# Gated merge of the two mixers with the activations stationary and tokens on partitions

## The chip, the core and the metric

The kernel runs on one core of a Trainium2 chip. The metric is the device time of one execution in microseconds (us); runs of one kernel are given by their median. TensorE is called PE, its weight load PEld, VectorE DVE, ScalarE ACT; SP is the queue that issues the transfers.

## The reference

One transformer block on x of 256 tokens by 2048 features, in f32. What matters here:

```python
z = h @ w_in                                  # h: normed and modulated x
q, kc, vc, ks, vs, kw, vw, g_nsa, lx, ly, ga, gb = jnp.split(z, ...)
o_a = nsa_attention(...)                      # 256 x 2048
o_b = jax.nn.gelu(ly) * rg_lru(u, ...)        # 256 x 2048
merged = jax.nn.sigmoid(ga) * (o_a @ proj_a) + jax.nn.sigmoid(gb) * (o_b @ proj_b)
return merged @ w_out
```

The merge is four products of 256 x 2048 by 2048 x 2048 (ga, gb, and the two projections), two sigmoids, two multiplications and a sum. The modulation vector behind h comes from `ada_w`, 96 pieces of 1 MB.

## The kernel before, in words

Every f32 product is made of three products of a faster format: both operands are split into a rounded part (hi) and the rest (lo), and hi hi, hi lo and lo hi are added in PSUM. An activation tile holds both parts side by side, 256 tokens of hi and 256 of lo, features on partitions. Weights come in 1 MB pieces through a ring of four `raw` tiles (`stage`, L97); ACT rounds each half piece (1024 columns) into `hi` (L107) and DVE writes the rest into `lo` (L108). There are three buffers of `hi` and three of `lo`, so a half piece is split while PE works three halves earlier. A half piece is 12 or 16 matmuls on PE.

Three forms of product matter. `dense_pair` (L114) holds 128 x 128 blocks of weights in the array and streams activations: the hi block sees 512 columns (256 tokens' hi and lo, L130), the lo block 256 (L131); the two 256-wide halves of the PSUM bank are added by DVE in `reduce` (L226). Its result has features on partitions. `dense_tok` (L191) holds 128 tokens of the activations and streams 512 columns of weights: three matmuls of 512 (L202 to L204). Its result has tokens on partitions and needs no `reduce`; `w_out` and `w_down` use it. `dense_pair1` (L171) is a form of three matmuls of 256 (L184 to L187), used by the recurrent mixer (LRU) ahead of the merge.

The first third of the program is made of passes over contraction blocks (`SPANS`, four of them): in each pass `tiles_of` (L408) adds a few blocks of the contraction to twelve output tiles, because h itself is still being made. Blocks 8 and 9 (`VB`) are products with tokens on partitions (L419 to L421); all others, the two gate blocks `mq` (10 and 11) among them, are three matmuls of 256 columns (L426 to L428). `out_of` (L430) adds each pass to the SBUF tile. The `mq` blocks are the first 512 columns of ga and gb.

The merge (L735 to L758) runs over eight groups of 256 columns. For each mixer s it makes the gate (`dense_pair` of `w_gates`, or `mq` for the first two groups), its sigmoid, the projection (`dense_pair` of `w_proj`), and the product of both; the sum is split into `mg` (features on partitions), which `dense_tok` of `w_out` (L789) reads as the stationary side. Behind each mixer come one or two `filler` pieces: a 1 MB piece of `ada_w` is loaded into the same ring and DVE multiplies and sums it (L233, then a short L234). `to_row` (L264) is a small transpose.

The order on each engine is set when the program is built, by a scheduler with a model of time; the transfers on SP stay in the order of the code. At run time an engine takes its instructions strictly in that order, each waiting for its semaphores.

Of the kernel before, what the change touches and what calls it, by code (L numbers as in the profile page):

```python
# [5 lines left out]
F32 = mybir.dt.float32  # L6
F32R = mybir.dt.float32r
BF16 = mybir.dt.bfloat16
AF = mybir.ActivationFunctionType
ALU = mybir.AluOpType  # L10
# [3 lines left out]
T = 256  # L14
# [24 lines left out]
def block_kernel(tc, x_t, x_n, gf_row, cols_d, consts_d, ada_w, w_kv0, w_kv, w_v, w_gate, w_q, cmp_w, cmp_w2,  # L39
# [16 lines left out]
    with ExitStack() as es:  # L56
# [167 lines left out]
        def reduce(out_ap, p):  # L224
            with tc.high_priority(200):
                V.tensor_reduce(out_ap, p.rearrange("p (a b) -> p b a", a=2), axis=AX, op=ALU.add)  # L226
# [23 lines left out]
        for c in range(4):  # L250
            p = bank()
# [137 lines left out]

        held = {}  # L390

        mq = [big.tile([128, 4, T], F32, tag="M%d" % n, name="mq") for n in range(2)]

        blocks = [(w_kv[i], kvc[i] if i < 2 else kT[:, i - 2]) for i in range(4)]
        blocks += [(w_q[i], qT[i]) for i in range(4)]
        blocks += [(w_v[b], vN[:, b]) for b in range(2)]
        blocks += [(w_mq[i], mq[i]) for i in range(2)]
        KV, Q, VB, MQ = range(4), range(4, 8), range(8, 10), range(10, 12)

        def banks_of(i, q):  # L400
            if i > 1:
# [6 lines left out]
        def tiles_of(i, ps, hi, lo, c0, kt, q):  # L408

            k0, k1 = SPANS[q] if i > 1 else (0, KT)  # L410
            first, last = kt == k0, kt == k1 - 1
            if q == 2 and i > 3 and i % 2:
                first, last = kt == k1 - 2, kt == k1 - 3
            if i in VB:
                wh, wl = hi[:, c0:c0 + 512], lo[:, c0:c0 + 512]
                for j in range(2):
                    xh = h1[:, kt, j * 128:j * 128 + 128]
                    xl = h1[:, kt, 256 + j * 128:256 + j * 128 + 128]
                    PE.matmul(ps[j], xh, wh, start=first, stop=False, skip_group_check=True)  # L419
                    PE.matmul(ps[j], xh, wl, start=False, stop=False, skip_group_check=True)  # L420
                    PE.matmul(ps[j], xl, wh, start=False, stop=last, skip_group_check=True)  # L421
                return
            for f in range(4):
                o = ps[f // 2][:, (f % 2) * 256:(f % 2) * 256 + 256]
                sl = slice(c0 + f * 128, c0 + f * 128 + 128)
                PE.matmul(o, hi[:, sl], h1[:, kt, 0:256], start=first and f % 2 == 0, stop=False, skip_group_check=True)  # L426
                PE.matmul(o, hi[:, sl], h1[:, kt, 256:512], start=False, stop=False, skip_group_check=True)  # L427
                PE.matmul(o, lo[:, sl], h1[:, kt, 0:256], start=False, stop=last, skip_group_check=True)  # L428

        def out_of(i, ps, q):  # L430
            if i < 2 and q < 3:
                return
            for j in range(2):
                dst = blocks[i][1]
                if i in VB:
                    v, d = ps[j], dst[:, j]
                else:
                    v, d = ps[j].rearrange("p (f t) -> p f t", f=2), dst[:, 2 * j:2 * j + 2]
                if q == 0 or i < 2:
                    A.activation(d, v, AF.Copy)  # L440
                else:
                    V.tensor_tensor(d, v, d, op=ALU.add)
# [34 lines left out]
        def filler(n=1):  # L477
            for _ in range(n):
                if fill:
                    m, kt = fill.pop(0)  # L480
                    ada_piece(crow, ada_w[m, kt], m * 16 + kt)
# [250 lines left out]
        for n in (4, 5):  # L732
            m2 = big.tile([128, 2, 2, 512], F32R, tag="D%d" % n, name="mg2")
            mg += [m2[:, 0], m2[:, 1]]
        for gr in range(8):  # L735
            m = []
            for s, rhs in ((0, lambda kt: oA[:, kt]), (1, lambda kt: oB[kt // 2][:, kt % 2])):
                if gr < 2:
                    sg = mq[s][:, 2 * gr:2 * gr + 2]
                else:  # L740
                    ps = dense_pair([w_gates[gr - 2, s, k] for k in range(2)], h1r)
                    sg = tmp.tile([128, 2, 256], F32, tag=("r", "iu")[s], bufs=1, name="sg")
                    for f in range(2):
                        reduce(sg[:, f], ps[f])
                A.activation(sg, sg, AF.Sigmoid)
                ps = dense_pair([w_proj[gr, s, k] for k in range(2)], rhs)
                pv = tmp.tile([128, 2, 256], F32, tag="tt", bufs=1, name="pv")
                for f in range(2):
                    reduce(pv[:, f], ps[f])
                V.tensor_tensor(sg, sg, pv, op=ALU.mult)  # L750
                m.append(sg)
                filler(1 if gr < 2 else 2)
            if gr == 5:
                row1 = to_row(32)
            V.tensor_tensor(m[0], m[0], m[1], op=ALU.add)
            oh = mg[gr][:, :, 0:256]
            A.activation(oh, m[0], AF.Copy)
            V.tensor_tensor(mg[gr][:, :, 256:512], m[0], oh.bitcast(F32), op=ALU.subtract)  # L758
        filler(max(0, len(fill) - 16))


# [120 lines left out]
def _pack(w, c=256, k=8):  # L882
    K, N = w.shape
    return np.ascontiguousarray(w.reshape(K // (128 * k), k, 128, N // c, c).transpose(3, 0, 2, 1, 4)).reshape(
        N // c, K // (128 * k), 128, k * c)
# [19 lines left out]
def _layout(i):  # L905
    f = {k: np.asarray(v) for k, v in i.items()}
    a = {}
    a["x_t"] = np.ascontiguousarray(f["x"][0].T.reshape(KT, 128, T).transpose(1, 0, 2))
    a["x_n"] = np.ascontiguousarray(f["x"][0].reshape(2, 128, D).transpose(1, 0, 2))
    a["gf_row"] = f["final_g"]  # L910
    parts = [_colv(f["c"]), _colv(f["ada_b"]), _colv(f["norm1_g"]), _colv(f["norm2_g"]),
             _colv(f["lru_conv_b"]), _colv(f["lru_conv_w"]), _colv(f["lru_ba"]), _colv(f["lru_bi"]),
             _colv(f["lru_lambda"]), _colv(f["ffn_conv_b"]), _colv(f["ffn_conv_w"]), 
             np.full((128, 1), EPS, np.float32), np.eye(128, dtype=np.float32)]
    cols = np.zeros((128, NCOLS), np.float32)
    cols[:, :_off] = np.concatenate(parts, axis=1)
    a["cols"] = cols
    qp = np.arange(128)
    causal = np.where(qp[None, :] <= qp[:, None], 0.0, NEG)
    vis = (np.arange(NCMP) * 16 + 31)[None, :] <= np.arange(T)[:, None]  # L920
    vis4 = np.repeat(vis.reshape(2, 128, 1, NCMP), 4, axis=2).transpose(1, 0, 2, 3).reshape(128, 120)
    a["consts"] = np.concatenate([causal, np.where(vis4, 0.0, NEG), vis4.astype(np.float64)],
                                 axis=1).astype(np.float32)
    a["consts"] = np.concatenate([a["consts"], f["cmp_pos_k"][0].T, f["cmp_pos_v"][0].T], axis=1)
    ada = f["ada_w"][0]
    a["ada_w"] = np.ascontiguousarray(ada.T).reshape(6, KT, 128, D)
    a["ada_w"][1, 0] = ada[:, D:D + 128].reshape(KT, 128, 128).transpose(1, 0, 2).reshape(128, D)
    w = f["w_in"][0]
    kv = np.concatenate([w[:, 2048:3072], w[:, 3072:3584], w[:, 4096:4608]], axis=1)
    a["w_kv0"] = kv[:256].reshape(2, 128, 2048)  # L930
    a["w_kv"] = _blocks(kv)
    a["w_v"] = _blocks(np.concatenate([w[:, 3584:4096], w[:, 4608:5120]], axis=1))
    a["w_gate"] = np.ascontiguousarray(w[:, 5120:5168].reshape(KT, 128, 48).transpose(1, 0, 2)).reshape(128, 768)
    a["w_q"] = _blocks(w[:, 0:2048])
    a["cmp_w"] = np.stack([np.ascontiguousarray(f[n][0].transpose(1, 0, 2)).reshape(128, 4096)
                           for n in ("cmp_w1_k", "cmp_w1_v")])
    a["cmp_w2"] = np.stack([f["cmp_w2_k"][0], f["cmp_w2_v"][0]], axis=1)
    a["w_lru"] = np.concatenate([_pack(w[:, 5168:7216]), _pack(w[:, 7216:9264])])
    lw = np.stack([f["lru_wa"][0], f["lru_wi"][0]], axis=1).reshape(4, 4, 2, 128, 128)
    a["lru_w"] = np.ascontiguousarray(lw.transpose(0, 3, 1, 2, 4)).reshape(4, 128, 1024)  # L940
    ga, gb = w[:, 9264:11312], w[:, 11312:13360]
    a["w_mq"] = np.concatenate([_blocks(ga[:, :512]), _blocks(gb[:, :512])])
    a["w_gates"] = np.stack([_pack(ga[:, 512:]), _pack(gb[:, 512:])], axis=1)
    a["w_proj"] = np.stack([_pack(f["proj_a"][0]), _pack(f["proj_b"][0])], axis=1)
    a["w_out"] = _tok(f["w_out"][0])
    up = f["ffn_up"][0]
    a["w_up"] = np.stack([_pack(up[:, :DFF]).reshape(2, 12, 2, 128, 2048),
                          _pack(up[:, DFF:]).reshape(2, 12, 2, 128, 2048)], axis=2)
    dn = f["ffn_down"][0]
    a["w_down"] = np.stack([_tok(dn[:DFF // 2]), _tok(dn[DFF // 2:])])  # L950
    return {k: np.ascontiguousarray(v) for k, v in a.items()}
# [17 lines left out]
```

## Time and profile before

| | us |
|---|---|
| median of 3 runs (1819.79 to 1822.76) | 1820.9 |
| the profiled execution, its own time | 1822.74 |
| its span, from the first to the last instruction | 1820.9 |
| PE busy | 1799.7 (99%) |
| DVE busy | 1372.0 (75%) |
| ACT busy | 868.2 (48%) |

The profiled execution lies 1.8 us above the median. PE counts as busy from the start of a matmul to its modelled end, so matmuls that overlap count once, and the rate of the work is read from the starts of matmuls, not from busy time. The merge stands from about 600 to 922 us of the span, `w_out` from 919 to 1009, the passes from about 30 to 340.

### The profile page before, as it was taken

The page shows a single profiled execution, that of the slowest core. Times are in us where ns is not written, and L with a number is a line of the kernel's source. Part 1 is how long each engine was busy: PE and PEld are TensorE (multiplying, and loading weights), DVE is VectorE, ACT ScalarE, POOL GpSimd, SP SyncE. Part 2 cuts the span into 40 slices and gives each one's busy share as a digit, 9 for nine tenths or more (in the row PEclk, how much of TensorE's full clock was granted, in tenths as well). Part 3 has the DMA queues.
Part 4 walks back from the last instruction along what each step waited for, and adds up shares of the span by engine and source line. Part 5 has one row for each costly group of instructions (what it writes and reads, how often), then busy time and mean ns, then how long its engine had stood idle before and what let it go on. Part 6 is the DMA issues. An engine that isn't in the chain of part 4 may idle for free.

```text
span 1820.9 us, 27160 instructions
## 1 busy us (share of the span) xinstructions
PE 1799.7 (99%) x10952; PEld 1586.8 (87%) x10952; DVE 1372.0 (75%) x1990; ACT 868.2 (48%) x1168; POOL 0.2 (0%) x4
## 2 busy tenths in 40 slices
PE   8999999999999999999999999999999999999998
PEld 7999998788999888888888998888888888888886
DVE  7998866888788877777766898888654677777555
ACT  5644534655578444444445554444433444444443
POOL 0000000000000000000000000000000000000000
PEclk9999999999999999999999999999999999999999
DMA  9999862555756677777776566777655555555553
GB/s 350 371 332 349 316 237 103 193 201 185 253 204 229 248 262 281 284 279 283 283 263 208 172 225 244 259 280 277 254 193 200 185 185 187 187 191 190 194 186 114
DMA packets 64206, 429.60 MB, mean 236 GB/s; under 512 B 7088, under 2 KB 7376, under 8 KB 15568
## 3 DMA queue, kind: packets, MB, share of 16 engines
q1 hardware_dynamic: 63792, 427.08, 66.3%
q8 instruction: 86, 1.41, 0.3%
q10 hardware_dynamic: 288, 0.79, 0.1%
q14 instruction: 40, 0.33, 0.1%
HBM read 425.72 MB, written 2.11 MB: 235 GB/s over the span
## 4 chain that ended last, share of the span: by engine, by line
PE 96%; DVE 1%; ACT 1%; issue 1%; DMA 1%; DVEq 0%; ACTq 0%
PE P L130 29%; PE P L131 15%; PE P L204 6%; PE P L202 6%; PE P L203 6%; PE P L426 3%; PE P L428 3%; PE P L427 3%; PE P L184 3%; PE P L187 3%; PE P L186 3%; PE P L148 1%; PE P L147 1%; PE P L149 1%; PE s L621 1%; PE oT L651 1%
## 5 line engine op out<-in xcount | busy, mean ns | idle before, releaser
L107 ACT ACTIVATE hi<-raw 128x1024 fp32r<-128x1024 f32 x589 | 623.4, 1060 | 812.1 <-PE P L130 401.3
L108 DVE TENSOR_TENSOR lo<-raw,hi 128x1024 fp32r<-128x1024 f32 x589 | 717.3, 1221 | 368.5 <-ACT hi L107 367.2
L130 PE MATMUL P<-h,hi 128*128 128x512 f32 x1728 | 599.9, 396 | 0.0
L131 PE MATMUL P<-h,lo 128*128 128x256 f32 x1728 | 468.2, 280 | 0.0
L130 PEld LDWEIGHTS P<-h,hi 128*128 128x128 f32 x1728 | 318.0, 188 | 69.2
L131 PEld LDWEIGHTS P<-h,lo 128*128 128x128 f32 x1728 | 326.0, 189 | 8.8
L233 DVE SCALAR_TENSOR_TENSOR raw<-raw,crow 128x2048 f32<-128x2048 f32 x64 | 146.2, 2284 | 1.8 <-DMA raw<-ada_w 1.7
L184 PE MATMUL P<-h,hi 128*128 128x256 f32 x512 | 146.8, 287 | 0.7 <-ACT hi L107 0.7
L187 PE MATMUL P<-h,lo 128*128 128x256 f32 x512 | 147.3, 288 | 0.1
L186 PE MATMUL P<-h,hi 128*128 128x256 f32 x512 | 146.9, 287 | 0.0
L426 PE MATMUL P<-h,hi 128*128 128x256 f32 x512 | 144.0, 285 | 0.0
L427 PE MATMUL P<-h,hi 128*128 128x256 f32 x512 | 143.4, 284 | 0.0
L428 PE MATMUL P<-h,lo 128*128 128x256 f32 x512 | 137.3, 284 | 0.0
L187 PEld LDWEIGHTS P<-h,lo 128*128 128x128 f32 x512 | 97.9, 191 | 3.3 <-issue 2.5
L184 PEld LDWEIGHTS P<-h,hi 128*128 128x128 f32 x512 | 97.9, 191 | 2.3 <-ACT hi L107 1.3
L426 PEld LDWEIGHTS P<-h,hi 128*128 128x128 f32 x512 | 98.5, 192 | 0.4
L186 PEld LDWEIGHTS P<-h,hi 128*128 128x128 f32 x512 | 97.9, 191 | 1.1 <-issue 1.0
L427 PEld LDWEIGHTS P<-h,hi 128*128 128x128 f32 x512 | 98.5, 192 | 0.1
L428 PEld LDWEIGHTS P<-h,lo 128*128 128x128 f32 x512 | 94.5, 192 | 1.6 <-issue 1.5
L203 PE MATMUL P<-lo,ua 128*128 128x512 f32 x240 | 93.4, 389 | 0.0
L204 PE MATMUL P<-hi,ua 128*128 128x512 f32 x240 | 93.4, 389 | 0.0
L130 PE MATMUL P<-oA,hi 128*128 128x512 f32 x256 | 90.2, 402 | 0.0
(254 smaller groups left out, 2789.3 us busy)
## 6 DMA issues: line engine op xcount, KB each, us to landing
raw<-ada_w SPq DMA_DIRECT2D x96, 1024.0 KB, 4.9
raw<-w_up SPq DMA_DIRECT2D x96, 1024.0 KB, 5.0
raw<-w_down SPq DMA_DIRECT2D x48, 1024.0 KB, 4.9
raw<-w_lru SPq DMA_DIRECT2D x32, 1024.0 KB, 5.0
raw<-w_proj SPq DMA_DIRECT2D x32, 1024.0 KB, 6.0
raw<-w_gates SPq DMA_DIRECT2D x24, 1024.0 KB, 5.5
raw<-w_out SPq DMA_DIRECT2D x16, 1024.0 KB, 5.2
raw<-w_kv SPq DMA_DIRECT2D x24, 512.0 KB, 6.7
```

The lines of the kernel that those rows point to most:

```text
L107: A.activation(hi[:, :n], raw[:, lo_col:lo_col + n], AF.Copy)
L108: V.tensor_tensor(lo[:, :n], raw[:, lo_col:lo_col + n], hi[:, :n].bitcast(F32), op=ALU.subtract)
L130: PE.matmul(ps[f], hi[:, sl], r, start=(kt == 0), stop=False, skip_group_check=True)
L131: PE.matmul(o, lo[:, sl], r[:, 0:256], start=False, stop=(kt == n - 1), skip_group_check=True)
L184: PE.matmul(o, hi[:, sl], r[:, 0:256], start=(kt == 0 and f == 0), stop=False, skip_group_check=True)
L186: PE.matmul(o, hi[:, sl], r[:, 256:512], start=False, stop=False, skip_group_check=True)
L187: PE.matmul(o, lo[:, sl], r[:, 0:256], start=False, stop=(kt == n - 1), skip_group_check=True)
L203: PE.matmul(ps[j], xh, lo[:, w], start=False, stop=False, skip_group_check=True)
L204: PE.matmul(ps[j], xl, hi[:, w], start=False, stop=(kt == n - 1), skip_group_check=True)
L426: PE.matmul(o, hi[:, sl], h1[:, kt, 0:256], start=first and f % 2 == 0, stop=False, skip_group_check=True)
L427: PE.matmul(o, hi[:, sl], h1[:, kt, 256:512], start=False, stop=False, skip_group_check=True)
L428: PE.matmul(o, lo[:, sl], h1[:, kt, 0:256], start=False, stop=last, skip_group_check=True)
```

## The change

The merge runs over four groups of 512 columns, and its gates and projections are made by `dense_tok`. Gate and projection stay in PSUM: ACT takes the sigmoid from there (L746), DVE multiplies from there (L749). The sum has tokens on partitions, so PE transposes it in blocks of 128 x 128 (L760, 32 of them), and ACT and DVE split each transposed block from PSUM into `mg` (L762, L763). The two `mq` blocks of the passes join the `TOK` branch. The fillers are the same 28 pieces, now two or four in a row; the weights of gates and projections are laid out in pieces of 512 columns.

```diff
--- before.py
+++ after.py
@@ -389,13 +389,13 @@
 
         held = {}
 
-        mq = [big.tile([128, 4, T], F32, tag="M%d" % n, name="mq") for n in range(2)]
+        mq = [big.tile([128, 2, 512], F32, tag="M%d" % n, name="mq") for n in range(2)]
 
         blocks = [(w_kv[i], kvc[i] if i < 2 else kT[:, i - 2]) for i in range(4)]
         blocks += [(w_q[i], qT[i]) for i in range(4)]
         blocks += [(w_v[b], vN[:, b]) for b in range(2)]
         blocks += [(w_mq[i], mq[i]) for i in range(2)]
-        KV, Q, VB, MQ = range(4), range(4, 8), range(8, 10), range(10, 12)
+        KV, TOK = range(4), range(8, 12)
 
         def banks_of(i, q):
             if i > 1:
@@ -411,7 +411,7 @@
             first, last = kt == k0, kt == k1 - 1
             if q == 2 and i > 3 and i % 2:
                 first, last = kt == k1 - 2, kt == k1 - 3
-            if i in VB:
+            if i in TOK:
                 wh, wl = hi[:, c0:c0 + 512], lo[:, c0:c0 + 512]
                 for j in range(2):
                     xh = h1[:, kt, j * 128:j * 128 + 128]
@@ -432,7 +432,7 @@
                 return
             for j in range(2):
                 dst = blocks[i][1]
-                if i in VB:
+                if i in TOK:
                     v, d = ps[j], dst[:, j]
                 else:
                     v, d = ps[j].rearrange("p (f t) -> p f t", f=2), dst[:, 2 * j:2 * j + 2]
@@ -732,30 +732,35 @@
         for n in (4, 5):
             m2 = big.tile([128, 2, 2, 512], F32R, tag="D%d" % n, name="mg2")
             mg += [m2[:, 0], m2[:, 1]]
-        for gr in range(8):
+        for n in range(4):
             m = []
             for s, rhs in ((0, lambda kt: oA[:, kt]), (1, lambda kt: oB[kt // 2][:, kt % 2])):
-                if gr < 2:
-                    sg = mq[s][:, 2 * gr:2 * gr + 2]
+                if n == 0:
+                    sg = [mq[s][:, j] for j in range(2)]
+                    ps = sg
                 else:
-                    ps = dense_pair([w_gates[gr - 2, s, k] for k in range(2)], h1r)
-                    sg = tmp.tile([128, 2, 256], F32, tag=("r", "iu")[s], bufs=1, name="sg")
-                    for f in range(2):
-                        reduce(sg[:, f], ps[f])
-                A.activation(sg, sg, AF.Sigmoid)
-                ps = dense_pair([w_proj[gr, s, k] for k in range(2)], rhs)
-                pv = tmp.tile([128, 2, 256], F32, tag="tt", bufs=1, name="pv")
-                for f in range(2):
-                    reduce(pv[:, f], ps[f])
-                V.tensor_tensor(sg, sg, pv, op=ALU.mult)
+                    ps = dense_tok([w_gates[n - 1, s, k] for k in range(4)], h1r)
+                    sg = [tmp.tile([128, 512], F32, tag=(("r", "iu"), ("u", "tt"))[s][j], bufs=1, name="sg")
+                          for j in range(2)]
+                for j in range(2):
+                    A.activation(sg[j], ps[j], AF.Sigmoid)
+                ps = dense_tok([w_proj[n, s, k] for k in range(4)], rhs)
+                for j in range(2):
+                    V.tensor_tensor(sg[j], ps[j], sg[j], op=ALU.mult)
                 m.append(sg)
-                filler(1 if gr < 2 else 2)
-            if gr == 5:
+                filler(2 if n == 0 else 4)
+            if n == 2:
                 row1 = to_row(32)
-            V.tensor_tensor(m[0], m[0], m[1], op=ALU.add)
-            oh = mg[gr][:, :, 0:256]
-            A.activation(oh, m[0], AF.Copy)
-            V.tensor_tensor(mg[gr][:, :, 256:512], m[0], oh.bitcast(F32), op=ALU.subtract)
+            for j in range(2):
+                V.tensor_tensor(m[0][j], m[0][j], m[1][j], op=ALU.add)
+            for f in range(4):
+                kt = 4 * n + f
+                p = psx.tile([128, 512], F32, tag="s", bufs=2, name="turn")
+                for j in range(2):
+                    PE.transpose(p[:, j * 128:j * 128 + 128], m[0][j][:, f * 128:f * 128 + 128], ident)
+                d = mg[kt // 2][:, kt % 2]
+                A.activation(d[:, 0:256], p[:, 0:256], AF.Copy)
+                V.tensor_tensor(d[:, 256:512], p[:, 0:256], d[:, 0:256].bitcast(F32), op=ALU.subtract)
         filler(max(0, len(fill) - 16))
 
 
@@ -940,8 +945,8 @@
     a["lru_w"] = np.ascontiguousarray(lw.transpose(0, 3, 1, 2, 4)).reshape(4, 128, 1024)
     ga, gb = w[:, 9264:11312], w[:, 11312:13360]
     a["w_mq"] = np.concatenate([_blocks(ga[:, :512]), _blocks(gb[:, :512])])
-    a["w_gates"] = np.stack([_pack(ga[:, 512:]), _pack(gb[:, 512:])], axis=1)
-    a["w_proj"] = np.stack([_pack(f["proj_a"][0]), _pack(f["proj_b"][0])], axis=1)
+    a["w_gates"] = np.stack([_tok(ga[:, 512:]), _tok(gb[:, 512:])], axis=1)
+    a["w_proj"] = np.stack([_tok(f["proj_a"][0]), _tok(f["proj_b"][0])], axis=1)
     a["w_out"] = _tok(f["w_out"][0])
     up = f["ffn_up"][0]
     a["w_up"] = np.stack([_pack(up[:, :DFF]).reshape(2, 12, 2, 128, 2048),
```

Where the schedule moves, at three places (the names: `lt` tiles of the LRU, `oB` its output, `raw`, `hi`, `lo` as above, numbers are those of the build). First, DVE at the end of the LRU, up to the `lo` of the first half piece of the merge (`raw_6489` before, `raw_6298` in the change). Before:

```order
L108 TENSOR_TENSOR lo_6362<-raw_6359,hi_6361 128x1024
L108 TENSOR_TENSOR lo_6390<-raw_6359,hi_6389 128x1024
L713 SCALAR_TENSOR_TENSOR lt_6182<-lt_6181,lt_6182 128x1024
L108 TENSOR_TENSOR lo_6420<-raw_6417,hi_6419 128x1024
L714 TENSOR_TENSOR lt_6182<-lt_6182 128x1024
L108 TENSOR_TENSOR lo_6448<-raw_6417,hi_6447 128x1024
L233 SCALAR_TENSOR_TENSOR raw_6577,modc_93<-raw_6577,crow_125 128x2048
L716 SCALAR_TENSOR_TENSOR lt_6182<-lt_6181,lt_6182 128x256 x4
L108 TENSOR_TENSOR lo_6492<-raw_6489,hi_6491 128x1024
```

and in the change:

```order
L108 TENSOR_TENSOR lo_6170<-raw_6167,hi_6169 128x1024
L713 SCALAR_TENSOR_TENSOR lt_5990<-lt_5989,lt_5990 128x1024
L108 TENSOR_TENSOR lo_6198<-raw_6167,hi_6197 128x1024
L714 TENSOR_TENSOR lt_5990<-lt_5990 128x1024
L108 TENSOR_TENSOR lo_6228<-raw_6225,hi_6227 128x1024
L716 SCALAR_TENSOR_TENSOR lt_5990<-lt_5989,lt_5990 128x256 x4
L108 TENSOR_TENSOR lo_6256<-raw_6225,hi_6255 128x1024
L722 TENSOR_TENSOR lt_5989<-lt_5989,lt_5990 128x512
L108 TENSOR_TENSOR lo_6301<-raw_6298,hi_6300 128x1024
```

The filler's L233 no longer stands ahead of the first `lo` of the merge; L722 does, and the second half of the last LRU piece but one (`lo_6198`, before `lo_6390`) stands behind L713 and no longer ahead of it.

Second, DVE around one group of four fillers, behind the projection of a group and ahead of the next gate (`raw_6828` and `raw_6862` are the last two pieces of the projection, `raw_6916` the first piece of the gate). In the change:

```order
L233 SCALAR_TENSOR_TENSOR raw_6898,modc_93<-raw_6898,crow_125 128x2048
L108 TENSOR_TENSOR lo_6831<-raw_6828,hi_6830 128x1024
L234 TENSOR_TENSOR modc_93<-modc_93,cols_113 128x1
L108 TENSOR_TENSOR lo_6847<-raw_6828,hi_6846 128x1024
L233 SCALAR_TENSOR_TENSOR raw_6902,modc_93<-raw_6902,crow_125 128x2048
L108 TENSOR_TENSOR lo_6865<-raw_6862,hi_6864 128x1024
L233 SCALAR_TENSOR_TENSOR raw_6906,modc_93<-raw_6906,crow_125 128x2048
L234 TENSOR_TENSOR modc_93<-modc_93,cols_113 128x1
L108 TENSOR_TENSOR lo_6881<-raw_6862,hi_6880 128x1024
L233 SCALAR_TENSOR_TENSOR raw_6910,modc_93<-raw_6910,crow_125 128x2048
L234 TENSOR_TENSOR modc_93<-modc_93,cols_113 128x1
L108 TENSOR_TENSOR lo_6919<-raw_6916,hi_6918 128x1024
```

and before, around a group of two fillers:

```order
L233 SCALAR_TENSOR_TENSOR raw_7052,modc_93<-raw_7052,crow_125 128x2048
L758 TENSOR_TENSOR mg_6481<-mq_205,mg_6481 128x2x256
L108 TENSOR_TENSOR lo_6967<-raw_6964,hi_6966 128x1024
L234 TENSOR_TENSOR modc_93<-modc_93,cols_113 128x1
L108 TENSOR_TENSOR lo_6987<-raw_6964,hi_6986 128x1024
L233 SCALAR_TENSOR_TENSOR raw_7056,modc_93<-raw_7056,crow_125 128x2048
L226 TENSOR_REDUCE sg_6958<-P_6872 128x256
L226 TENSOR_REDUCE sg_6958<-P_6873 128x256
L108 TENSOR_TENSOR lo_7009<-raw_7006,hi_7008 128x1024
```

Four fillers now stand among five splits, where two stood among three; the reductions are gone.

Third, PE at the transposes (here the first two of the eight of a group): they stand 26 matmuls behind the start of the next group's first product. In the change:

```order
L202 MATMUL P_7234<-hi_7272,h1_169 128x512
L202 MATMUL P_7235<-hi_7272,h1_169 128x512
L760 MATMUL turn_7214<-cols_113,sg_6754 128x128
L760 MATMUL turn_7219<-cols_113,sg_6754 128x128
L203 MATMUL P_7234<-lo_7273,h1_169 128x512
L204 MATMUL P_7234<-hi_7272,h1_169 128x512
L202 MATMUL P_7234<-hi_7272,h1_169 128x512
L203 MATMUL P_7234<-lo_7273,h1_169 128x512
```

Two more stand 38 matmuls and four 67 matmuls behind the same start; before, the next product's matmuls follow each other there without them.

## Rows read from the trace of the kernel before

**Rows 1.** The page's busy time by engine, whole span.
```profile
PE 1799.7 (99%) x10952; PEld 1586.8 (87%) x10952; DVE 1372.0 (75%) x1990; ACT 868.2 (48%) x1168; POOL 0.2 (0%) x4
```

**Rows 2.** Busy time by window: stretch, length, PE, PEld, DVE, ACT, POOL, clock, DMA share, GB/s.
```profile
40.00:60.00 20.00, 18.87 (x131) 17.02 (x131) 16.20 (x16) 15.92 (x28) 0.00 (x0) 1.00 0.98 362
700.00:750.00 50.00, 50.00 (x287) 43.55 (x286) 40.33 (x48) 20.65 (x21) 0.00 (x0) 1.00 0.79 286
600.00:607.00 7.00, 5.25 (x23) 4.28 (x23) 7.00 (x11) 2.06 (x3) 0.00 (x0) 0.76 0.73 262
946.00:951.50 5.50, 5.50 (x28) 4.57 (x27) 3.57 (x6) 2.85 (x4) 0.00 (x0) 1.00 0.56 191
```

**Rows 3.** Timeline of PE: start, us, line; two first matmuls of attention's projection, 48 half pieces apart.
```profile
750.41 0.62 PE L130 MATMUL P<-oA,hi 128*128 128x512 f32 x2
885.17 0.62 PE L130 MATMUL P<-oA,hi 128*128 128x512 f32 x2
```

**Rows 4.** Timeline of PE in the passes: 48 matmuls of 512, then 24 of 256.
```profile
106.94 0.63 PE L419 MATMUL P<-hi,h 128*128 128x512 f32 x2
117.84 0.28 PE L426 MATMUL P<-h,hi 128*128 128x256 f32 x1
120.72 0.28 PE L426 MATMUL P<-h,hi 128*128 128x256 f32 x1
```

**Rows 5.** Timeline of PE at the start of the merge (in brackets: idle before, and releaser).
```profile
600.66 0.63 PE L130 MATMUL P<-oA,hi 128*128 128x512 f32 x2
603.04 0.39 PE L131 MATMUL P<-oA,lo 128*128 128x256 f32 x1 [1.75 <-DVE lo L108]
607.03 0.63 PE L130 MATMUL P<-oA,hi 128*128 128x512 f32 x2
47.40 0.99 PE L419 MATMUL P<-hi,h 128*128 128x512 f32 x2 [0.69 <-ACT hi L107]
```

**Rows 6.** Timeline of DVE and ACT at the same place.
```profile
597.23 2.29 DVE L233 SCALAR_TENSOR_TENSOR raw<-raw,crow 128x2048 f32<-128x2048 f32 x1
599.44 2.43 DVE L716 TENSOR_TENSOR_SCAN lt<-lt 128x256 f32<-128x256 f32 x4
601.79 1.20 DVE L108 TENSOR_TENSOR lo<-raw,hi 128x1024 fp32r<-128x1024 f32 x1
602.98 0.68 DVE L722 TENSOR_TENSOR lt<-lt 128x512 f32<-128x512 f32 x1
591.04 1.06 ACT L711 ACTIVATE lt<-lt 128x1024 f32<-128x1024 f32 x1
592.14 1.23 DVE L713 SCALAR_TENSOR_TENSOR lt<-lt 128x1024 f32<-128x1024 f32 x1 [3.51 <-ACT lt L711]
593.28 1.22 DVE L108 TENSOR_TENSOR lo<-raw,hi 128x1024 fp32r<-128x1024 f32 x1
```

**Rows 7.** Timeline of PE in w_out: four transposes among matmuls of 512.
```profile
946.13 0.62 PE L202 MATMUL P<-hi,mg 128*128 128x512 f32 x2
946.59 0.60 PE L798 MATMUL turn<-cols,res 128*128 128x128 f32 x4
947.26 0.39 PE L204 MATMUL P<-hi,mg 128*128 128x512 f32 x1
```

**Rows 8.** All work on the transposed tiles of w_out: count, ns min/median/max.
```profile
L798 PE MATMUL turn<-cols,res x32: 270/272/273, 946.6 to 1018.3; 128*128 128x128 f32 x32
```

**Rows 9.** Timeline in the merge: ACT's split, and a filler on DVE up to its successor.
```profile
753.32 1.06 ACT L107 ACTIVATE hi<-raw 128x1024 fp32r<-128x1024 f32 x1 [1.76 <-PE P L130]
744.32 2.28 DVE L233 SCALAR_TENSOR_TENSOR raw<-raw,crow 128x2048 f32<-128x2048 f32 x1
746.53 0.69 DVE L758 TENSOR_TENSOR mg<-sg,mg 128x512 fp32r<-128x512 f32 x1
747.13 1.22 DVE L108 TENSOR_TENSOR lo<-raw,hi 128x1024 fp32r<-128x1024 f32 x1
748.27 0.15 DVE L234 TENSOR_TENSOR modc<-modc,cols 128x1 f32<-128x1 f32 x1
```

**Rows 10.** DMA issues: KB each, median us to landing.
```profile
raw<-ada_w SPq DMA_DIRECT2D x96, 1024.0 KB, 4.9
```

## The prediction

> **What bounds the kernel now.** Start with the page's busy time [rows 1]: PE is busy 99% of the span, DVE 75%, ACT 48%. Busy time of overlapping matmuls hides their rate, so the next view is the windows [rows 2]: in the middle of the merge (700 to 750) PE is busy without a gap while DVE has 10 us of 50 free and the 16 DMA engines a fifth of their time. So in the merge the end is set by how fast PE can start matmuls, and an edit counts there by the PE time that it takes or adds, unless it makes PE wait. Two stretches are different. At 40 to 60 us the transfers are at 98% and PE has gaps. At 600 to 607 PE is busy for 5.25 of 7 us and its granted clock averages 0.76: something is late there. The rates come from the timeline, from one start to another.
>
> **The weights' form in the merge.** From 750.41 to 885.17 PE does 48 half pieces of weights in the paired form [rows 3]: 134.76 / 48 = 2.81 us each. Each is eight matmuls of 512 columns and eight of 256. The new form does the same half piece with twelve of 512: as many columns, four matmuls and four loads fewer. Its rate stands in the passes, at the same clock and with transfers and DVE as busy: 48 matmuls of 512 from 106.94 to 117.84 [rows 4], 10.90 us, 2.725 per half piece. The difference is 0.083 us. The merge has four groups, two projections each of eight halves (64), and three groups with two gates (48): 112 halves, so **-9.3 us**. It could be nothing, if attention's or the LRU's output as the stationary side were slower than h is in the passes. I see no reason for that in an instruction of the same shape.
>
> **The gate blocks in the passes.** Their half piece is 24 matmuls of 256, 2.88 us from 117.84 to 120.72 [rows 4], and becomes twelve of 512, 2.725: 0.155 less. There are 2 x 8 halves. The two of the first pass lie where PE waits for transfers [rows 2], and save nothing; 14 x 0.155 = **-2.2 us**. Bounds: 0, if the transfers became the limit in the later passes too, and -2.5.
>
> **The transposes.** 32 are new on PE. w_out has 32 of the same shape. Between the starts at 946.13 and 947.26 [rows 7] lie two matmuls of 512 from the pair, a third one, and four transposes; three matmuls are 0.68, so four transposes cost 1.13 - 0.68 = 0.45. 32 cost **+3.6 us**. The record of one is 272 ns long [rows 8], but records overlap; 32 x 0.272 = 8.7 would be the upper bound, if each stood alone. The Trainium skill (TensorE: Matmul & The Clock Gate, Part 4, PE-mode transpose) gives some 275 ns for a transpose inside a kernel; by that figure the transposes would cost 8.8 us and the sum would be 5.2 us worse, and the trace agrees with the length of the record but not with this as a price.
>
> PE waits at a transpose only if DVE's sum is late. The first two transposes stand 26 matmuls, 5.9 us, behind the start of the next product. By then DVE has to do two products from PSUM, two sums (0.69 each, like L758 in [rows 9]) and three splits of 1.14 at most: 6.2 us if nothing ran ahead, but the first split is done before the product starts (below), so about 5. I take no wait. In the last group the blocks transposed last, at 67 matmuls, are read by w_out at 84, 3.9 us later; ACT and DVE need some 2.2.
>
> **Work taken off DVE and ACT.** 56 reductions go, 16 passes over 512 columns become products from PSUM, the final split doubles in count at half the size. DVE had free time there, PE none [rows 2]: nothing.
>
> **Four fillers in a row.** This is where a wait can come in, at six places. A filler's transfer, its 1 MB in the ring and its 2.2 us on DVE stand ahead of the splits. Set 0 at the start of the gate behind the fillers, 2.725 us per half. ACT starts a split 5.4 before the half is due: the one at 753.32 [rows 9] is for the half that PE starts at 758.8. DVE needs 2.2 per filler and 1.14 per split, from start to next start [rows 9]. The first transfer is released by the split of the projection's second half, at -22.1, and lands 4.9 later [rows 10], -17.2. From -16.6 DVE goes: filler to -14.4, split to -13.2; the next split waits for ACT until -12.5, done -11.3; filler -9.1, split -8.0, filler -5.8, split -4.6, filler -2.4, split of the gate's first half -1.2, with the short L234s -1.0. The gate's first transfer goes into the second filler's buffer, leaves at -9.0 and lands at about -4, in time. So the split that PE needs at 0 is done 1.0 before. I take **0**; the bound on the other side is in the rivals.
>
> **The start of the merge.** Before, DVE does a filler at 597.23, then four scans, then the first `lo` of the merge at 601.79 [rows 6]. PE starts at 600.66, waits 1.75 us for it, and then runs at the lower level of its clock (1.2 GHz, 2.4 being full) up to 607 [rows 2, 5]: the first half takes 6.37 instead of 2.81, **3.6 us lost**, half by the wait and half by the clock. In the new order the filler stands behind that split. Without its 2.2 us, and with L722's 0.6 in its place, the split would start at 600.2 and be done at 601.3, about when PE asks for it. But another split moves the other way: the half that is due 8.4 us (70 matmuls of 0.12) before the merge now stands behind L711 and L713. L711 ends 8.6 before the merge [rows 6]; with one ACT split (1.06) fewer ahead of it, 9.6. Add L713 and the split (592.14 to 594.4, 2.3): 7.3 against 8.4, so PE waits 1.1 there. A wait of 0.69 left the clock up [rows 5] and 1.00 in that window [rows 2], one of 1.75 did not; 1.1 is a little nearer to the former. With the clock's 1.8 it would cost 2.9, without 1.1; I take 1.6. The gain is 3.6 - 1.6 = **-2.0 us**; bounds 0 and -3.6.
>
> **Sum.** -9.3 - 2.2 + 3.6 - 2.0 = -9.9. The profiled execution, 1822.7, becomes 1812.8. The median of the runs lies 1.8 below it, at 1820.9, so I forecast **1811.0 us**. About 0.2% (3.6 us) is what a measurement of this kernel can tell from no change; the line to that is 1817.3.
>
> **Rivals.**
> - *The stall at the merge stays, or moves whole to the LRU's last halves* (-2.0 goes, up to +1 more): 1813.0 to 1814.0. For it: the new late split; against: the filler is gone from the path. Still faster. Chance 0.15.
> - *The fillers are late.* If the split of the gate's first half is 1.0 us later than worked out, PE begins to wait at each of six places. Up to 1.7 us of wait each leaves at most +10, 1821: chance 0.10, with half of it below the line. From 2.7 us later on, each wait is as long as that at 603.04 [rows 5], the clock falls too, and each costs 3.6: +21.6, **1832.6, slower**. It takes a transfer that lands at 7.6 instead of 4.9 us or splits held up behind a filler that waits. For it: two or three 1 MB transfers are in flight there; against: the buffers' releases are 2 to 5 us apart, and DMA has room [rows 2]. Chance 0.04.
> - *The transposes let the clock fall.* If each of the eleven places where they stand cost what the clock cost at the start of the merge, 1.8 us, that is +20: 1831. Against: four of them in a row left the clock at 1.00 in the window from 946 [rows 2]. Chance 0.02. The Trainium skill (same page, Part 4) says that transposes do not count as work that holds the full clock; the trace shows no fall beside such short groups.
> - *No gain from the form*: if half pieces took 2.81 in the merge as before, 1820.3, no change. For it: the columns are as many; against: [rows 4]. Chance 0.04.
> - *The change does not do what it says*: excluded, the schedule shows the new matmuls, transposes and fillers in place.
>
> **How the numbers follow.** The forecast has 0.65. It spans 1807 (all of the stall gone, all of the passes' gain, a run at the fast end) to 1814; with the first rival and the milder part of the second, the range that should hold 8 times in 10 is 1806 to 1817. Faster than 1817.3: 0.65 + 0.15 + 0.05 = 0.85. Within 0.2%: half the milder filler rival and the fourth, 0.09. Slower: 0.06.
>
> **What the profile after would show.** In the merge, matmuls of 512 only, starts 0.227 apart, 2.72 to 2.73 per half; no L226 there. 32 transposes at 0.11 each between matmuls, clock at 1.00. At the merge's start no wait of over 1 us on a `lo`, and perhaps one of about 1 some 8 us ahead of it. At the six filler places no PE wait for `lo`. DVE's busy time 30 to 40 us less. I am wrong if half pieces in the merge take 2.8 us, if PE waits for a `lo` behind fillers, or if the clock reads below 1.00 at those places.

## The result, and the profile after

The changed kernel takes 1811.67 us (median of 13 runs, 1809.89 to 1819.07), the kernel before 1822.09 us on the same occasion (13 runs). The ratio is 0.9947, with a 95% interval of 0.9938 to 0.9956: 8 to 11 us less. The forecast was 1811.0 us and 9.9 us less. The profiled execution took 1810.84 us.

The page's busy time by engine, as in [rows 1]:

```profile
PE 1788.1 (99%) x10344; PEld 1555.3 (86%) x10344; DVE 1338.8 (74%) x1942; ACT 867.3 (48%) x1176; POOL 0.2 (0%) x4
```

PE has 608 matmuls fewer, DVE 33 us less work. That is as the change says: 112 x 4 + 16 x 12 fewer by the wider matmuls, 32 more by the transposes. As in [rows 1], the 99% says little; the windows (columns as in [rows 2]) and the starts of matmuls tell the rest.

```profile
40.00:60.00 20.00, 18.64 (x106) 15.65 (x105) 16.18 (x17) 16.11 (x28) 0.00 (x0) 1.00 0.98 370
700.00:750.00 50.00, 49.89 (x223) 40.83 (x223) 34.53 (x39) 20.89 (x24) 0.00 (x0) 1.00 0.77 274
597.00:604.00 7.00, 7.00 (x33) 5.81 (x33) 3.94 (x5) 4.18 (x5) 0.00 (x0) 1.00 0.77 261
```

In the first 7 us of the merge, 597 to 604 now, PE is busy all the time at clock 1.00; in [rows 2] it was 5.25 of 7 at 0.76. In the middle of the merge PE is no longer quite without a gap (49.89 of 50).

PE's timeline: the merge's first half piece, one of attention's projections (eight halves), four transposes at the start of a group, and the waits in the LRU and the merge.

```profile
597.06 0.40 PE L202 MATMUL P<-hi,oA 128*128 128x512 f32 x1
599.81 0.39 PE L202 MATMUL P<-hi,oA 128*128 128x512 f32 x1
...
751.85 0.39 PE L202 MATMUL P<-hi,oA 128*128 128x512 f32 x1
773.61 0.61 PE L202 MATMUL P<-hi,h 128*128 128x512 f32 x2
...
646.05 0.62 PE L202 MATMUL P<-hi,h 128*128 128x512 f32 x2
646.51 0.60 PE L760 MATMUL turn<-cols,mq 128*128 128x128 f32 x4
...
564.70 0.39 PE L187 MATMUL P<-h,lo 128*128 128x256 f32 x1 [1.50 <-DVE lo L108]
...
818.26 0.51 PE L203 MATMUL P<-lo,h 128*128 128x512 f32 x1 [0.50 <-DVE lo L108]
```

- *The form.* (773.61 - 751.85) / 8 = 2.720 us for a half piece, 2.8075 before [rows 3]. All ten products of the merge that are neither the first nor hold transposes run at this pace. 112 halves: 9.8 us less.
- *The start of the merge.* The first half takes 2.75 us (597.06 to 599.81), 6.37 before [rows 5]. 3.6 us less, no residue there.
- *The transposes.* A product that holds eight of them (640.61 to 663.32, 22.71) is 0.95 longer than one without (21.76): 0.12 each. The three groups inside the merge and the last one in `w_out` make 3.8 us more.
- *The passes, attention and the LRU.* From the wait at 47.40 (46.95 after) to the start of the merge it takes 553.3 before and 550.1 after, 3.1 us less. Not all of it is the passes: PE waits 0.7 us in the LRU before (0.28 at 570.42 and 0.44 at 571.36) and 2.1 after (0.56 at 528.07 and 1.50 at 564.70).
- *The fillers.* The second and third product with transposes (from 728.60 and 817.13) take 23.25 and 23.58 in place of 22.71: 0.5 and 0.9 us of waits, 1.4 together.

The sum: -9.8 - 3.6 + 3.8 - 3.1 + 1.4 = -11.3; the profiled executions differ by 11.9, of which 0.45 lie ahead of that first wait, and the medians by 10.4.

### The profile page after: what moved, and what is told of

Its sections match the earlier page's. It is cut to its first block, busy times and chain, and to the rows that moved or that the text cites. A ratio compares the mean times of both kernels' runs of the same rounds, so it can differ in the third digit from the quotient of the medians.

```text
span 1809.0 us, 25836 instructions
## 1 busy us (share of the span) xinstructions
PE 1788.1 (99%) x10344; PEld 1555.3 (86%) x10344; DVE 1338.8 (74%) x1942; ACT 867.3 (48%) x1176; POOL 0.2 (0%) x4
## 4 chain that ended last, share of the span: by engine, by line
PE 94%; DVE 3%; DMA 1%; ACT 1%; issue 1%; DVEq 0%; ACTq 0%
PE P L130 17%; PE P L203 11%; PE P L204 11%; PE P L202 11%; PE P L131 9%; PE P L187 3%; PE P L184 3%; PE P L186 3%; PE P L426 2%; PE P L428 2%; PE P L427 2%; PE P L420 2%; PE P L421 2%; PE P L419 1%; PE P L148 1%; PE P L147 1%
## 5 line engine op out<-in xcount | busy, mean ns | idle before, releaser
L130 PE MATMUL P<-h,hi 128*128 128x512 f32 x1344 | 465.9, 397 | 0.0
L131 PE MATMUL P<-h,lo 128*128 128x256 f32 x1344 | 362.8, 280 | 0.0
L130 PEld LDWEIGHTS P<-h,hi 128*128 128x128 f32 x1344 | 246.7, 188 | 53.2
L131 PEld LDWEIGHTS P<-h,lo 128*128 128x128 f32 x1344 | 253.6, 189 | 7.7
L233 DVE SCALAR_TENSOR_TENSOR raw<-raw,crow 128x2048 f32<-128x2048 f32 x64 | 146.3, 2286 | 13.0 <-DMA raw<-ada_w 13.0
L187 PE MATMUL P<-h,lo 128*128 128x256 f32 x512 | 147.1, 288 | 2.1 <-DVE lo L108 2.1
L184 PE MATMUL P<-h,hi 128*128 128x256 f32 x512 | 146.7, 287 | 0.0
L186 PE MATMUL P<-h,hi 128*128 128x256 f32 x512 | 146.6, 286 | 0.0
L426 PE MATMUL P<-h,hi 128*128 128x256 f32 x384 | 108.0, 286 | 0.0
L427 PE MATMUL P<-h,hi 128*128 128x256 f32 x384 | 107.3, 284 | 0.0
L428 PE MATMUL P<-h,lo 128*128 128x256 f32 x384 | 102.2, 284 | 0.0
L187 PEld LDWEIGHTS P<-h,lo 128*128 128x128 f32 x512 | 97.7, 191 | 3.9 <-DVE lo L108 2.6
L184 PEld LDWEIGHTS P<-h,hi 128*128 128x128 f32 x512 | 97.9, 191 | 3.3 <-issue 3.0
L186 PEld LDWEIGHTS P<-h,hi 128*128 128x128 f32 x512 | 97.9, 191 | 1.1 <-issue 1.0
L203 PE MATMUL P<-lo,ua 128*128 128x512 f32 x240 | 93.4, 389 | 0.0
L204 PE MATMUL P<-hi,ua 128*128 128x512 f32 x240 | 93.4, 389 | 0.0
L202 PE MATMUL P<-hi,ua 128*128 128x512 f32 x240 | 83.6, 389 | 0.0
L203 PE MATMUL P<-lo,h 128*128 128x512 f32 x192 | 75.5, 393 | 0.6 <-DVE lo L108 0.5
L204 PE MATMUL P<-hi,h 128*128 128x512 f32 x192 | 74.9, 390 | 0.0
L426 PEld LDWEIGHTS P<-h,hi 128*128 128x128 f32 x384 | 74.1, 193 | 0.2
```

The costliest lines, as they stand in the source:

```text
L130: PE.matmul(ps[f], hi[:, sl], r, start=(kt == 0), stop=False, skip_group_check=True)
L131: PE.matmul(o, lo[:, sl], r[:, 0:256], start=False, stop=(kt == n - 1), skip_group_check=True)
L184: PE.matmul(o, hi[:, sl], r[:, 0:256], start=(kt == 0 and f == 0), stop=False, skip_group_check=True)
L186: PE.matmul(o, hi[:, sl], r[:, 256:512], start=False, stop=False, skip_group_check=True)
L187: PE.matmul(o, lo[:, sl], r[:, 0:256], start=False, stop=(kt == n - 1), skip_group_check=True)
L202: PE.matmul(ps[j], xh, hi[:, w], start=(kt == 0), stop=False, skip_group_check=True)
```

## The experiments

Two questions were open: whether the gain is that of the form, and of what in it; and what the smaller terms (transposes, start, passes, fillers) weigh by themselves. Each ratio is to the kernel before, run on the same chip.

| run | median, us | ratio (95% interval) |
|---|---|---|
| e1_change_again | 1811.12 | 0.9945 (0.9932 to 0.9957) |
| e2_cut | 1818.97 | 0.9986 (0.9977 to 0.9995) |
| e3_spread | 1810.25 | 0.9936 (0.9923 to 0.9950) |
| e4_no_turn | 1806.89 | 0.9921 (0.9907 to 0.9934) |
| e5_filler_moved | 1819.29 | 0.9986 (0.9978 to 0.9995) |
| e6_passes_only | 1818.03 | 0.9977 (0.9967 to 0.9987) |
| e7_merge_only | 1813.51 | 0.9961 (0.9949 to 0.9973) |
| e8_eight | 1848.26 | 1.0146 (1.0128 to 1.0163) |
| e9_spread_again | 1810.55 | 0.9936 (0.9922 to 0.9950) |
| e10_change_again | 1811.29 | 0.9947 (0.9934 to 0.9959) |

The kernel before had 1821.77 us beside e1 to e4, 1822.11 beside e5 to e8, 1821.95 beside e9 and e10.

**e1: the changed kernel, as the reference of the next three.**

> The changed kernel as it is, on the same chip as the three edits of it that follow, so that they can be set against it. Expected 0.9947 of the kernel before, as measured first (about 1812 us); every theory says the same.

10.65 us less than before: the first result again.

**e2: the numbers of the paired form, activations still stationary.** In the merge's products of the changed kernel (shortened):

```diff
-PE.matmul(ps[j], xl, hi[:, w], ...)
+for c in range(2):
+    v = slice(k * 512 + 256 * c, k * 512 + 256 * c + 256)
+    PE.matmul(ps[j][:, 256 * c:256 * c + 256], xl, hi[:, v], ...)
```

> In the merge of the changed kernel the third matmul of each triple, 512 columns, is cut into two of 256: a half piece is then 8 matmuls of 512 and 8 of 256, the numbers of the paired form, but with activations still stationary. Theory (the gain of the form is the smaller number of PE instructions): a half piece takes 2.80 to 2.81 us as in the paired form and no longer 2.72, 112 halves are 9 to 10 us more, about 1821 us. Rival (the gain comes from which side is stationary, or from where the operands lie): half pieces stay at 2.72, no change from the changed kernel, 1812 us.

7.85 us more than e1. PE's timeline, two starts eight halves apart:

```profile
756.39 0.62 PE L202 MATMUL P<-hi,oA 128*128 128x512 f32 x2
778.74 0.63 PE L202 MATMUL P<-hi,h 128*128 128x512 f32 x2
```

22.35 / 8 = 2.793 per half: 0.073 more than in the change, 8.2 us in 112 halves. So most of the 9.8 us is the number of instructions, not the side that is stationary. (Each matmul has its weight load, so the two are not told apart.) A matmul of 512 takes 2.720 / 12 = 0.2267; the eight of 256 take (2.793 - 8 x 0.2267) / 8 = 0.122 each, 0.009 more than half of that. What remains, 0.0145 per half and 1.6 us in all, is of another kind: before, the halves of the gates take 2.80 and those of the projections 2.82 (11.19 and 11.27 for four; the step from 750.41 to 761.68 is one of the latter). Why the projections were slower wasn't tried; e5 below shows that it isn't their operands alone.

**e4: without the transposes.** In place of `psx.tile` and `PE.transpose`:

```diff
+p = m[0][f // 2][:, f % 2 * 256:f % 2 * 256 + 256]
```

> The changed kernel without its 32 transposes: the splits read the sum as it lies, with tokens on partitions, so the operand of w_out is left untransposed. Theory (four transposes cost PE 0.45 us, one 0.11): 3.6 us less, about 1808 us. Rival (a transpose costs the length of its record, 0.27 us): 8.7 us less, 1803 us. Rival (they fill gaps of PE, or the matmuls beside them hide them): no change, 1812 us.

4.2 us less than e1. That is near the 3.6 of the theory and far from the 8.7 of the rival. The product at the same place is down to the pace of the others (PE's timeline):

```profile
642.65 0.39 PE L202 MATMUL P<-hi,h 128*128 128x512 f32 x1
...
664.41 0.39 PE L202 MATMUL P<-hi,oA 128*128 128x512 f32 x1
```

21.76 us, 0.95 less than 22.71. The record of a transpose, 0.272 us, is not its price; 0.12 is.

**e3 and e9: fillers in twos.**

```diff
 ps = dense_tok([w_gates[n - 1, s, k] for k in range(4)], h1r)
+filler(2)
...
-filler(2 if n == 0 else 4)
+filler(2)
```

> The changed kernel with the same 28 fillers, but two behind each gate and two behind each projection in place of four behind each projection. Theory (four in a row make ACT's first split of the gate late at two of the places, where the trace shows PE's third matmul 0.44 and 0.82 us late): both waits go, 1.3 us less, about 1810.5 us, and no wait of PE on a lo in the merge. Rival (the transfers are what is late there, and the same bytes are asked for either way): the waits stay or move behind the gates, 1812 us.

> The kernel with the fillers in twos once more, beside the changed kernel on one chip, since the first pair of ratios (0.9936 and 0.9945) lie within each other's intervals. Theory (the waits at the fillers' places, 1.0 to 1.3 us, are gone): 1.0 to 1.3 us less than the changed kernel again, about 1810.3 us. Rival (the first difference was scatter of the runs): equal medians, 1811.3 us.

> The changed kernel beside it, for the comparison: 0.9945 of the kernel before, about 1811.3 us, by every theory.

0.87 and 0.74 us less than the changed kernel beside it. Each pair's intervals overlap, so the times alone don't settle it; the traces do. All waits of PE in e9 (columns: who waits for what; us in total, times, longest):

```profile
PE P L254 <- DVE dg L252: 4.8, 1, 4.8
PE hold L426 <- ACT h L291: 2.2, 1, 2.2
PE P L187 <- DVE lo L108: 1.2, 2, 0.7
PE hold L428 <- DVE lo L108: 0.7, 2, 0.5
PE P L419 <- ACT hi L107: 0.7, 1, 0.7
PE P L420 <- DVE lo L108: 0.4, 1, 0.4
PE hold L426 <- ACT hi L107: 0.2, 1, 0.2
```

None is in the merge (its matmuls are L202 to L204), and its gate products with transposes take 22.70, 22.71 and 22.75. In the three profiles of the changed kernel the waits at fillers cost 1.4, 0.7 and 0.6 us. e3's own profiled execution (1814.42 us, the slowest of its five) also has none in the merge; in the passes it waited 2.29 us at 72.48, and behind that the clock averaged 0.60 up to 75 us. The medians of e3 and e9 are the lowest of the kernels that leave no work out, though the times alone don't tell them from the change.

**e5: the kernel before, with one filler a mixer later.**

```diff
-filler(1 if gr < 2 else 2)
+filler((0, 2, 1, 1)[2 * gr + s] if gr < 2 else 2)
```

> The kernel before with one edit: the filler behind the first projection of the merge comes one mixer later, so that its multiplication no longer stands ahead of the split of the merge's first half piece. No product changes its form. Theory (the 1.75 us wait and the low clock behind it are one loss of 3.6 us, made by that filler): the first half piece takes 2.81 us and not 6.37, about 1818.2 us. Rival (only the wait goes, the clock falls there anyway): 1.8 us less, 1820 us. Rival (the recurrent mixer's own work is late there, the filler not): no change, 1821.8 us.

2.8 us less, without any product in a new form. PE's timeline at the start of the merge, and its next two products:

```profile
599.89 0.39 PE L130 MATMUL P<-oA,hi 128*128 128x512 f32 x1
600.67 0.39 PE L131 MATMUL P<-oA,lo 128*128 128x256 f32 x1 [0.39 <-DVE lo L108]
...
611.84 0.40 PE L130 MATMUL P<-oB,hi 128*128 128x512 f32 x1
623.04 0.39 PE L130 MATMUL P<-oA,hi 128*128 128x512 f32 x1
```

and the window at the start, where [rows 2] has 5.25 and 0.76:

```profile
600.00:607.00 7.00, 6.62 (x38) 5.54 (x37) 5.32 (x6) 4.79 (x7) 0.00 (x0) 1.00 0.66 204
```

The first product takes 11.95, 14.81 before: 2.9 less, though the wait is shorter by only 1.36. The rest is the clock, which stays up. So wait and clock were one loss, and a filler's place was enough to make it. The second product, on the LRU's output, takes 11.20, no more than a gate's 11.19.

**e6: only the passes; e7: only the merge.** The lines that matter:

```diff
e6, in the kernel before:
-if i in VB:
+if i in TOK:    # range(8, 12)
...
-sg = mq[s][:, 2 * gr:2 * gr + 2]
+sg = mq[s][:, gr].rearrange("p (f t) -> p f t", f=2)
e7, in the changed kernel:
-KV, TOK = range(4), range(8, 12)
+KV, TOK = range(4), range(8, 10)
...
-sg = [mq[s][:, j] for j in range(2)]
+sg = [mq[s][:, 2 * j:2 * j + 2].rearrange("p f t -> p (f t)") for j in range(2)]
```

> The kernel before with the two gate blocks of the passes in the new form and the merge in the old one, which reads them as they lie (so the gates' first 512 columns go to wrong tokens; the work is the same). Theory (0.155 us per half piece, 14 to 16 of them): the passes end 2.2 to 2.5 us sooner; the filler still stands ahead of the merge's first split, so the stall there stays, 3.6 to 4.2 us: about 1819.5 us. Rival (transfers set the pace of the passes): no change, 1821.8 us.

> The changed kernel with the two gate blocks of the passes in the old form (the merge reads them as they lie, so the gates' first 512 columns go to wrong tokens). Theory (the parts add up: 9.6 us of the form less, 3.8 of transposes more, 1.3 of fillers more, 3.6 of the merge's start less): 8.0 to 8.2 us less than the kernel before, about 1813.7 us, 2.2 to 2.5 more than the changed kernel. Rival (the start of the merge is better only because the passes end sooner): the stall is back, 1817 us.

e7 is 8.6 us less than before and, by the differences to the kernel before, 2.05 more than the change, near the 2.2 to 2.5 that I expected. e6 is 4.1 less (2.4 to 6.0 by its interval), not the 2.2 to 2.5 expected; in its trace the stall at the merge shrank too, and the merge's first product takes 12.11 in place of 14.81. DVE, ACT and PE in e6:

```profile
584.88 1.06 ACT L711 ACTIVATE lt<-lt 128x1024 f32<-128x1024 f32 x1
...
585.97 1.23 DVE L713 SCALAR_TENSOR_TENSOR lt<-lt 128x1024 f32<-128x1024 f32 x1 [3.48 <-ACT lt L711]
...
594.59 2.29 DVE L233 SCALAR_TENSOR_TENSOR raw<-raw,crow 128x2048 f32<-128x2048 f32 x1
...
596.80 1.22 DVE L108 TENSOR_TENSOR lo<-raw,hi 128x1024 fp32r<-128x1024 f32 x1
...
596.88 0.63 PE L130 MATMUL P<-oA,hi 128*128 128x512 f32 x2
598.08 0.39 PE L131 MATMUL P<-oA,lo 128*128 128x256 f32 x1 [0.57 <-DVE lo L108]
```

The filler still stands ahead of the `lo`, but ACT's L711 starts 12.0 us ahead of the merge; before it was 9.6 (591.04 to 600.66, [rows 5, 6]). That order of ACT and DVE comes with the passes' part of the change. So either thing alone, the filler away (e5, e7) or the LRU's chain 2.4 us sooner (e6), leaves 0.4 to 0.6 us of the 1.75 at that place; the changed kernel has both, and no wait. That fits with e6 and e7 adding up to 12.7 us and the change to 10.4 to 10.7, since the stall can be removed once; but the intervals are wider than these 2 us, so the traces carry this, not the sum.

**e8: fillers in eights.**

```diff
-filler(2 if n == 0 else 4)
+filler((0, 4)[s] if n == 0 else (0, 8)[s])
```

> The changed kernel with the fillers eight in a row behind every second projection, in place of four behind each. Theory (the price of the rival that forecast slower: each filler takes a turn of 2.2 us on DVE and 1 MB of transfer, and PE has at most three half pieces ahead): PE waits at each of the three places for over 3 us on a hi or lo, and the clock falls behind it; 20 to 40 us more, 1832 to 1852 us. Rival (the ring and the idle time of the engines take that too): the same waits as with four, 1812 to 1814 us.

37 us more than e1 (two runs), inside the range, but not by the wait that I named. Timeline of PE and SP, and two windows:

```profile
735.14 0.66 PE L760 MATMUL turn<-cols,sg 128*128 128x128 f32 x2 [4.65 <-DVE sg L755]
737.93 0.69 PE L760 MATMUL turn<-cols,sg 128*128 128x128 f32 x2 [2.13 <-DVE sg L755]
740.10 1.22 PE L202 MATMUL P<-hi,h 128*128 128x512 f32 x2 [1.48 <-ACT hi L107]
...
730.87 9.57 SPq L53 DMA_DIRECT2D raw<-w_gates  x4
```

```profile
730.00:735.00 5.00, 0.48 (x3) 0.06 (x1) 5.00 (x10) 0.00 (x0) 0.00 (x0) 1.00 1.01 423
735.00:740.00 5.00, 1.35 (x4) 0.58 (x4) 5.00 (x5) 1.56 (x4) 0.00 (x0) 0.51 1.00 411
740.00:745.00 5.00, 4.90 (x13) 3.79 (x14) 5.00 (x12) 2.59 (x5) 0.00 (x0) 0.50 0.98 397
```

Most of it is at the transposes: the sums that they need stand among fillers on DVE. But the next gate's pieces leave SP only at 730.87, behind eight fillers, so PE would have had to wait there without transposes too (this was argued from the queue, not tried). PE is idle for 8 to 11 us at each of three places, and after it the clock is at its lower level. Eight behind one mixer are more than the ring and DVE take; four cost about 1 us.

## Why the prediction was right, and where it was off

The total came out within 1 us (9.9 forecast, 10.4 by the medians). That is in part luck: by the terms as the trace has them, the form, the passes and the start gained 0.5, 0.9 and 1.6 more than forecast, the transposes and the fillers cost 0.2 and 1.4 more, and these errors cancel in part. One sign that the prediction gave for being wrong did come: PE waits for a `lo` behind fillers (818.26).

- *The weights' form, -9.3*: 9.8 by the trace. The rate that the passes gave, 2.725, is 2.720 in the merge. That attention's and the LRU's outputs as the stationary side would be slower was ruled out rightly. That the cause is the number of matmuls is what e2 shows, for 0.073 of the 0.0875 per half.
- *The gate blocks in the passes, -2.2*: 2.6 of the 3.1 between the same points in the trace. The passes' own matmuls, summed from start to start without the waits, take 253.9 us before and 251.3 after. The two halves of the first pass were counted at nothing; with them the working gives 16 x 0.155 = 2.5. The rest of the 3.1 is not these blocks. PE's waits in this stretch are no shorter in all (2.7 before, 3.0 after): 0.5 shorter between 59 and 73 us (0.22 and 0.26 for 0.44 and 0.52), without attention's 0.63 at 346.61, and 1.3 longer in the LRU. Some 0.8 less lies in the matmuls of attention and the LRU, whose order moved too, and was not taken apart.
- *The transposes, +3.6*: 3.8 by the trace, 4.2 by e4. The price was read rightly from the spacing in w_out, and the clock stayed at 1.00. The figure of the Trainium skill (TensorE: Matmul & The Clock Gate, Part 4, PE-mode transpose), some 275 ns in bf16, is the length of a record in this trace too (272). e4 shows that it is not what one costs among matmuls.
- *The start of the merge, -2.0*: 3.6. The step that failed is the 1.6 us of residue at the last LRU block. It rested on L711 ending "9.6" before the merge, "with one ACT split (1.06) fewer ahead of it". ACT and DVE, after, as in [rows 6], and the same chain one block of the LRU sooner (560 to 565 us):

```profile
560.40 1.06 ACT L711 ACTIVATE lt<-lt 128x1024 f32<-128x1024 f32 x1
...
561.50 1.22 DVE L713 SCALAR_TENSOR_TENSOR lt<-lt 128x1024 f32<-128x1024 f32 x1 [1.18 <-ACT lt L711]
...
563.42 1.22 DVE L108 TENSOR_TENSOR lo<-raw,hi 128x1024 fp32r<-128x1024 f32 x1
...
585.07 1.06 ACT L711 ACTIVATE lt<-lt 128x1024 f32<-128x1024 f32 x1
...
586.16 1.23 DVE L713 SCALAR_TENSOR_TENSOR lt<-lt 128x1024 f32<-128x1024 f32 x1 [3.49 <-ACT lt L711]
587.30 1.22 DVE L108 TENSOR_TENSOR lo<-raw,hi 128x1024 fp32r<-128x1024 f32 x1
...
594.77 1.22 DVE L108 TENSOR_TENSOR lo<-raw,hi 128x1024 fp32r<-128x1024 f32 x1
```

  L711 ends 10.9 before the merge at 597.06, not 9.6: the next instruction on DVE starts at 586.16. So the split that I feared late is done at 588.4, and PE's first matmul that reads it starts at 588.57, with no wait listed. The mechanism was right, but it struck one block of the LRU sooner, which the working left out: there the `lo` starts at 563.42 behind L711 and L713, and PE waits 1.50 us for it at 564.70 (0.65 and 1.24 in the two other profiles of this kernel). The LRU's waits are 2.1 in all for 0.7 before. Set against the 3.6, the start gained 2.3 in this profile (3.1 and 2.5 in the two others), nearer to the 2.0 than the 3.6 is. e6 has these waits in the LRU and e7 has not, so they come with the passes' part of the change.
- *Four fillers in a row, 0*: 1.4, 0.7 and 0.6 us in three profiles. The working gave the first split of the gate 1.0 us of slack. By the timelines, from the end of DVE's split to PE's L203, it was 1.4, 0.7, 1.4 and 1.0 at four of the six places, and at two the split ended after PE's due start. The step that failed there is the gate's transfer, "lands at about -4, in time". DVE, SP and ACT ahead of the wait at 818.26:

```profile
807.06 2.29 DVE L233 SCALAR_TENSOR_TENSOR raw<-raw,crow 128x2048 f32<-128x2048 f32 x1 [1.01 <-DMA raw<-ada_w]
...
809.38 7.10 SPq L53 DMA_DIRECT2D raw<-w_gates  x4
...
815.89 2.01 ACT L107 ACTIVATE hi<-raw 128x1024 fp32r<-128x1024 f32 x2 [5.66 <-DMA raw<-w_gates]
...
816.98 1.23 DVE L108 TENSOR_TENSOR lo<-raw,hi 128x1024 fp32r<-128x1024 f32 x1 [0.78 <-ACT hi L107]
```

  The gate's first piece left at 809.38, 7.75 ahead of the product at 817.13 and not 9.0, right behind the end of a filler on DVE (L233) that had itself waited 1.01 for its transfer. It landed 6.5 us later, not 4.9, and so 1.2 ahead of the product. At the other late place it left 8.85 ahead, and ACT could split it only 7.2 us later; at three that were in time ACT started 5.1, 6.3 and 5.2 us after it left. Why one transfer takes longer than another was not tried. The page's median for these pieces, after:

```profile
raw<-w_gates SPq DMA_DIRECT2D x24, 1024.0 KB, 6.4
```

  In the kernel before it was 5.5:

```profile
raw<-w_gates SPq DMA_DIRECT2D x24, 1024.0 KB, 5.5
```

  I had taken the fillers' 4.9 [rows 10] for these too. This is the milder filler rival, at about a tenth of its upper price.
- *The rivals that ended slower* did not come: no place lost the clock in the merge. e8 shows that such a price exists when the cluster is doubled.

## What to carry to other kernels

When PE is bound by its own matmuls, count instructions: a product in fewer and wider matmuls gains by what each matmul costs above its columns (here a matmul of 256 takes 0.009 us more than half of one of 512), and its rate can be read from any place of the kernel that has the form already. Price small PE work by what it adds between the starts of its neighbours, not by the length of its record. For work that shares the ring and DVE, keep clusters short and place each behind a product of its own; and when an order changes, follow the late chain in every repetition of the block, not only in the last.

## What was not expected of the hardware

- A wait of 1.50 us at 564.70 left the granted clock at 1.00 afterwards; one of 1.75 at 603.04, before, was followed by 0.52. But in e4's profiled execution two shorter waits close together, 1.48 and 0.52, were followed by 0.50. The windows of the changed kernel, of the kernel before, and PE's timeline and a window of e4:

```profile
562.00:566.00 4.00, 2.50 (x22) 2.30 (x21) 4.00 (x7) 3.97 (x5) 0.00 (x0) 1.00 0.40 168
566.00:570.00 4.00, 4.00 (x36) 4.00 (x35) 4.00 (x7) 1.27 (x2) 0.00 (x0) 1.00 0.64 199
...
604.00:607.00 3.00, 3.00 (x11) 2.55 (x11) 3.00 (x4) 1.75 (x3) 0.00 (x0) 0.52 0.42 79
```

```profile
71.43 0.39 PE L426 MATMUL hold<-h,hi 128*128 128x256 f32 x1 [1.48 <-ACT hi L107]
...
72.69 0.58 PE L428 MATMUL hold<-h,lo 128*128 128x256 f32 x1 [0.52 <-DVE lo L108]
...
72.70:75.80 3.10, 3.10 (x14) 3.10 (x15) 2.56 (x3) 1.36 (x2) 0.00 (x0) 0.50 0.98 407
```

  For a single wait of 1.1 the prediction took 0.5 of the clock's 1.8; the single waits of 0.65, 1.24 and 1.50 at that place of the LRU cost none of it. What decides it was not measured.
- The paired form ran 0.02 us per half slower in the projections than in the gates (2.82 and 2.80), the new form equally fast in both (2.720). That attention's and the LRU's outputs are slower operands does not explain it: in e5 the second product of the merge, on the LRU's output, takes 11.20 for four halves (611.84 to 623.04), the pace of a gate. This stays open.
